# Expert gates built once and parked in DRAM, a longer lead of the u sides, and seven row buffers in a two-block transformer kernel

## The chip, the cores and the metric

One core of a Trainium2 chip runs the whole program in one launch. The metric is device time in microseconds for one execution. The core's engines are TensorE (PE, with its weight loads listed as PEld), VectorE (DVE), ScalarE (ACT), GpSimd (POOL) and SyncE (SP), and 16 DMA engines move data between DRAM and the on-chip memory, SBUF.

## What is computed

Two transformer blocks over 512 tokens of width 1024, in float32. The change lies in the first block's expert layer ("PEER"): 16384 experts, one row of `expert_u` and one of `expert_v` each, of which every token uses 16 for each of 8 heads.

```python
def block(xb):
    q = (xb @ w_query).reshape(PEER_TOKEN_BLOCK, PEER_HEADS, 2, PEER_HALF_DIM)
    s = jnp.einsum('chpd,hpnd->chpn', q, sub_keys).astype(jnp.float32)
    top_s, top_i = lax.top_k(s, PEER_TOPK)
    ...
    best_s, pos = lax.top_k(cand_s, PEER_TOPK)
    idx = jnp.take_along_axis(cand_i, pos, axis=-1)
    g = jax.nn.softmax(best_s, axis=-1)
    u = expert_u[idx]
    act = jax.nn.gelu(jnp.einsum('cd,chkd->chk', xb, u).astype(jnp.float32), approximate=False)
    w = (g * act).astype(xb.dtype)
    return jnp.einsum('chk,chkd->cd', w, expert_v[idx])
```

An expert's number is 128 i + j, with i and j the winners of two lists of 128 keys. Attention, norms and the second block's feed-forward are around it and are not touched, but for the buffers of the second block's attention result.

## The kernel before

Float32 products are made of three matmuls on a high and a low part (`mm3`). The high part `wh` of a weight tile is cut by ACT (L111), the low part `wl` by DVE or POOL (L112). Weights come in 256 KB tiles `wr` on SP's DMA queue (L93), a few tiles ahead.

The first 128 tokens take the **rows path**: for each of the 128 (head, choice) pairs, POOL issues an indirect DMA that fetches 128 rows of `expert_u` (`ur`, 512 KB; L1078), DVE multiplies them with the tokens and sums (L1081), and later the same is done with `expert_v` (`vr`), which DVE adds into `acc` (L1089). That makes 256 units; their buffers are the pool `prow`.

The other 384 tokens take the **dense path** over 128 expert blocks of 128 experts; block b holds the experts with i = b. A *u side* is 24 matmuls of 384 columns into PSUM (`pA`; the first twelve, made earlier, are called `pU`), and ACT's gelu. `weigh` (L1044 on) multiplies the result by the block's gates (`w`, DVE) and splits it (`wwh` on ACT, `wwl` on DVE). A *v side* is 18 matmuls of 512 columns into six PSUM banks `vac`, which hold the sum over all blocks.

The **gates** of a block are a 128 x 384 matrix over (j, token), mostly zeros. They are made for 8 tokens at a time (a *group*, 48 in all): DVE compares the chosen j and i with a row of numbers, which gives one-hot tiles `oj` and `oi` (L1000, float16), `oi` times the gate values gives `og` (L1007), and 16 matmuls per group multiply `oj` and `og` (`pG`, L1019 and L1020). ACT copies the result into a buffer `ring` (L1023) of 60 columns of 128 x 384, which the gelu results of the first blocks share. Since the ring does not hold all, the columns i are built in three chunks of 38, 45 and 45 (`CH`): the first before any v side, with ten u sides between; the second and third during the blocks 23 to 36 and 68 to 81 (`build`). In the first chunk every third group has its `og` made on POOL. The u sides lead the v sides by `AHEAD` = 22 blocks.

The main loop runs b over the blocks: u side of block b + 1 (from 22 on), v side of b, `weigh(b + 1)`, and then some gathers of the rows path, as many as the table `share` gives; each is settled by DVE at once. The program order fixes what each engine does in turn, together with a scheduler that orders instructions by when their inputs come; SP's queue holds loads in the order in which they are asked for.

Of the kernel before, what the change touches and what calls it, by code (L numbers as in the profile page):

```python
# [157 lines left out]
def body(ctx, tc, a):  # L158
# [276 lines left out]

    for b in range(P - KL):
        if b + 1 >= AHEAD:
            add_u(b + 1)
        add_v(b)
    for b in range(P - KL + 1, P):  # L440
        add_u(b)
    for b in range(P - KL, P):
# [548 lines left out]
    acc = pac.tile([P, D], FT, name="acc")
    starts = [sum(CH[:c]) for c in range(3)]

    def gate_hot(c, g):

        n, i0 = CH[c], starts[c]
        tt = slice(g * GS, (g + 1) * GS)

        def hot(out, q, j0, w):
            V.tensor_tensor(out, iT[:, q, tt].rearrange("p (s t) -> p s t", t=4)[:, :, None].to_broadcast([P, GS // 4, w, 4]),  # L1000
                            ioth[:, None, j0:j0 + w].to_broadcast([P, GS // 4, w, 4]), op=OP.is_equal)
        oj = pg.tile([P, GS // 4, P, 4], F16, name=f"oj{c}_{g}", tag="oj", bufs=3)
        hot(oj, 1, 0, P)
        oi = pg.tile([P, GS // 4, CW, 4], F16, name=f"oi{c}_{g}", tag="oi", bufs=2)
        hot(oi[:, :, :n], 0, i0, n)
        og = pg.tile([P, GS, 48], FT, name=f"og{c}_{g}", tag="og", bufs=3)
        (G if c == 0 and g % OGP == 0 else V).tensor_tensor(og[:, :, :n].rearrange("p (s t) i -> p s t i", t=4),  # L1007
                        oi[:, :, :n].rearrange("p s i t -> p s t i"),
                        gp32[:, tt].rearrange("p (s t) -> p s t", t=4)[:, :, :, None].to_broadcast([P, GS // 4, 4, n]),
                        op=OP.mult)  # L1010
        return c, g, oj, og

    def gate_sum(c, g, oj, og):
        n, i0 = CH[c], starts[c]
        tt = slice(g * GS, (g + 1) * GS)
        pt = ps.tile([P, GS, CW], FT, name=f"pG{c}_{g}", tag="pG")
        for t in range(GS):
            o = og[:, t, :n].bitcast(F16).rearrange("p (i w) -> p i w", w=2)
            T.matmul(pt[:, t, :n], oj[:, t // 4, :, t % 4], o[:, :, 1], start=True, stop=False)  # L1019
            last["pe"] = T.matmul(pt[:, t, :n], oj[:, t // 4, :, t % 4], o[:, :, 0], start=False, stop=True).ins  # L1020
        s0 = i0 % RING
        n1 = min(n, RING - s0)
        A.activation(ring[:, s0:s0 + n1, tt].rearrange("p i t -> p t i"), pt[:, :, :n1], AF.Copy)  # L1023
        if n1 < n:
            A.activation(ring[:, 0:n - n1, tt].rearrange("p i t -> p t i"), pt[:, :, n1:n], AF.Copy)

    hot = []
    late["tile"] = lambda n, tag, nm: pg.tile([P, n], FR, name=f"late{nm}", tag=tag, bufs=3)

    def gate_group(c, g, lag=2):  # L1030
        hot.append(gate_hot(c, g))
        if len(hot) > lag:
            gate_sum(*hot.pop(0))

    gact = {b: ring[:, CH[0] + b] for b in range(n_early)}

    def u_side(b):
# [3 lines left out]
        gact[b] = ring[:, CH[0] + b] if b < AHEAD else pg.tile([P, TD], FT, name=f"ga{b}", tag="ga")  # L1041
        last["gelu"] = A.activation(gact[b], pa_, AF.Gelu).ins  # L1042

    def weigh(b):  # L1044
# [1 line left out]
        V.tensor_mul(w, gact.pop(b), ring[:, b % RING])  # L1046
        if b < P - 2:
            wh, wl = (pg.tile([P, TD], FR, name=f"ww{c}{b}", tag=f"ww{c}") for c in "hl")
        elif b == P - 2:
            wh, wl = (late["tile"](TD, "og", f"w{c}") for c in "hl")  # L1050
        else:
            wh, wl = (pk.tile([P, TD], FR, name=f"late{c}", tag=c) for c in ("gp", "iT"))
# [4 lines left out]
    def v_side(*v):  # L1057

        for t in range(3):
            sl = slice(t * P, (t + 1) * P)  # L1060
            for b, wh, wl, vb in v:
                for n in range(2):
                    if hot and 2 * t + n in GAT:
                        with tc.issue_after(last["pe"]):
                            gate_sum(*hot.pop(0))
                    last["pe"] = mm3(vac[2 * t + n], wh[:, sl], wl[:, sl], vb[n][0], vb[n][1], b == 0, b == P - 1)
# [39 lines left out]
    NG = TD // GS  # L1106
    for i in range(NG):
        gate_group(0, i)
        NU = n_early
        if i * (AHEAD - NU) // NG != (i + 1) * (AHEAD - NU) // NG:  # L1110
            u_side(NU + i * (AHEAD - NU) // NG)
    while hot:
        gate_sum(*hot.pop(0))
# [4 lines left out]
    build = {}
    for c, (w0, w1) in ((1, (max(AHEAD, CH[0] + CH[1] - RING), CH[0] - 1)), (2, (P - RING, CH[0] + CH[1] - 1))):
        for i in range(NG):  # L1120
            build.setdefault(w0 + i * (w1 - w0) // NG, []).append((c, i))
    share = [SH_BUILD if b in build else (SH_EARLY if b < AHEAD else (SH_MID if b < 64 else SH_LATE if b < B_END else 0)) for b in range(P)]
    scale = len(units) / sum(share)
    due, done = 0.0, 0
# [460 lines left out]
```

## Time and profile before

| | us |
|---|---|
| median of 3 runs | 2203.68 (2198.78 to 2205.65) |
| the profiled execution | 2202.07 |
| its span | 2200.3 |
| PE busy in the span | 2090.5 |
| DVE busy | 1603.3 |
| ACT busy | 955.0 |
| POOL busy | 622.6 |

The profile is of one execution. The span is the time from the first to the last instruction. A matmul counts as busy from its start to its modelled end, so PE shown busy may still be at half its rate; the granted clock (PEclk, as a share of 2.4 GHz) tells which. The expert layer's stages follow one another: gates of the first chunk with ten u sides, v sides alone, the second chunk among u and v sides, u and v sides, the third chunk, u and v sides again, and a tail.

### The profile page before, as it was taken

To read this page: it belongs to the slowest core of one execution; us is meant where nothing else is said; L and a number is where in the kernel's file an instruction comes from. 1 tells how busy PE (TensorE), PEld (TensorE's weight loads), DVE (VectorE), ACT (ScalarE), POOL (GpSimd) and SP (SyncE) were. 2 spreads that over 40 slices of the span, in tenths; PEclk is the share of its full clock that TensorE was granted. 3 is DMA by queue.
4 is the path that set the end of the run, shared out by engine and by line. 5 is a ranking of instruction groups with operands and counts; after the bars stand their busy time and mean duration, and the time that the engine had idled before them with its cause. 6 is when DMAs were issued, how large, how long until landed. Compare 5 with 4: busy or idle time off the path is not lost.

```text
span 2200.3 us, 34912 instructions
## 1 busy us (share of the span) xinstructions
PE 2090.5 (95%) x12443; PEld 1768.9 (80%) x12443; DVE 1603.3 (73%) x3498; ACT 955.0 (43%) x1892; POOL 622.6 (28%) x537
## 2 busy tenths in 40 slices
PE   8999998978999999999999999999999999999999
PEld 5756787878888888888888878788878678888887
DVE  8789879988878987777899777777777855333322
ACT  4477342355445553333455433333453554333321
POOL 2245236664221123333311233333212420000000
PEclk9999999999999999999999999999999899999999
DMA  8525422331675558888855688888743121233332
GB/s 280 163 59 182 153 73 78 100 101 59 217 227 193 168 191 270 278 275 278 273 180 170 202 269 278 269 275 278 276 147 119 56 63 53 97 96 96 97 119 72
DMA packets 163633, 375.78 MB, mean 171 GB/s; under 512 B 18562, under 2 KB 22530, under 8 KB 163459
## 3 DMA queue, kind: packets, MB, share of 16 engines
q1 hardware_dynamic: 121058, 233.81, 31.9%
q0 software_dynamic: 36864, 134.23, 19.4%
q10 hardware_dynamic: 5536, 5.51, 0.9%
q8 instruction: 98, 1.61, 0.3%
q14 instruction: 77, 0.62, 0.1%
HBM read 366.66 MB, written 4.19 MB: 169 GB/s over the span
## 4 chain that ended last, share of the span: by engine, by line
PE 62%; DVE 14%; DMA 12%; issue 5%; ACT 3%; POOL 3%; SPq 0%; DVEq 0%; ACTq 0%; POOLq 0%
PE vac L200 5%; PE vac L199 5%; PE vac L201 5%; PE pA L199 4%; PE pA L200 4%; PE pA L201 4%; DMA vr<-in_v_dram,idx 4%; DMA ur<-in_u_dram,idx 3%; DMA wr<-in_uT_dram 3%; DMA wr<-in_v_dram 2%; PE pd L201 2%; PE pd L200 2%; PE pd L199 2%; PE upp L201 2%; PE upp L199 2%
## 5 line engine op out<-in xcount | busy, mean ns | idle before, releaser
L111 ACT ACTIVATE wh<-wr 128x512 fp32r<-128x512 f32 x716 | 447.8, 631 | 769.8 <-DMA wr<-in_v_dram 133.7
L112 DVE TENSOR_TENSOR wl<-wr,wh 128x512 fp32r<-128x512 f32 x640 | 429.9, 697 | 280.8 <-ACT wh L111 261.4
L200 PE MATMUL vac<-wl,wwh 128*128 128x512 f32 x756 | 305.2, 404 | 33.9 <-DVE wl L112 33.9
L199 PE MATMUL pA<-hA,wh 128*128 128x384 f32 x928 | 316.9, 342 | 0.0
L201 PE MATMUL pA<-hA,wl 128*128 128x384 f32 x928 | 313.8, 338 | 0.0
L200 PE MATMUL pA<-hA,wh 128*128 128x384 f32 x928 | 312.6, 337 | 0.0
L199 PE MATMUL vac<-wh,wwh 128*128 128x512 f32 x756 | 305.0, 404 | 0.6 <-ACT wwh L1053 0.5
L201 PE MATMUL vac<-wh,wwl 128*128 128x512 f32 x756 | 299.1, 396 | 0.1
L1078 POOL DMA_INDIRECT ur<-in_u_dram,idx x128 | 159.5, 1246 | 378.4 <-DVE acc L1089 304.1
L1078 POOL DMA_INDIRECT vr<-in_v_dram,idx x128 | 157.5, 1230 | 339.2 <-DVE ur L1081 265.3
L200 PEld LDWEIGHTS vac<-wl,wwh 128*128 128x128 f32 x756 | 144.6, 191 | 69.4 <-DVE wl L112 45.6
L1089 DVE SCALAR_TENSOR_TENSOR acc<-vr,act,acc 128x1024 f32<-128x1024 f32 x127 | 162.8, 1282 | 44.1 <-DMA vr<-in_v_dram,idx 42.9
L1081 DVE SCALAR_TENSOR_TENSOR ur<-ur,hn 128x1024 f32<-128x1024 f32 x128 | 156.3, 1221 | 43.5 <-DMA ur<-in_u_dram,idx 43.5
L199 PEld LDWEIGHTS pA<-hA,wh 128*128 128x128 f32 x928 | 176.2, 190 | 3.7 <-ACT ga L1042 0.3
L200 PEld LDWEIGHTS pA<-hA,wh 128*128 128x128 f32 x928 | 176.2, 190 | 3.1
L201 PEld LDWEIGHTS pA<-hA,wl 128*128 128x128 f32 x928 | 175.6, 189 | 0.0
L201 PEld LDWEIGHTS vac<-wh,wwl 128*128 128x128 f32 x756 | 144.3, 191 | 31.1 <-DVE wwl L1054 0.5
L199 PEld LDWEIGHTS vac<-wh,wwh 128*128 128x128 f32 x756 | 144.6, 191 | 28.7 <-ACT wwh L1053 0.6
L112 POOL TENSOR_TENSOR wl<-wr,wh 128x512 fp32r<-128x512 f32 x76 | 102.4, 1359 | 74.4 <-ACT wh L111 71.8
L1053 ACT ACTIVATE wwh<-w 128x384 fp32r<-128x384 f32 x126 | 66.0, 524 | 113.7 <-DVE w L1046 107.2
L1019 PEld LDWEIGHTS <-oj 128*128 128x128 f16 x1152 | 83.2, 117 | 38.3 <-issue 15.9
L1000 DVE TENSOR_TENSOR oj<-iT,ioth 128x1024 f16<-128x1024 f16 x144 | 106.5, 743 | 9.3 <-PE pG L1020 9.3
(697 smaller groups left out, 4294.3 us busy)
## 6 DMA issues: line engine op xcount, KB each, us to landing
wr<-in_uT_dram SPq DMA_DIRECT2D x256, 256.0 KB
wr<-in_v_dram SPq DMA_DIRECT2D x256, 256.0 KB
wa<-in_w_adaT_dram SPq DMA_DIRECT2D x48, 512.0 KB
wr<-in_w_gate_dram SPq DMA_DIRECT2D x44, 256.0 KB
wr<-in_w_up_dram SPq DMA_DIRECT2D x44, 256.0 KB
wr<-in_w_down_dram SPq DMA_DIRECT2D x44, 256.0 KB
wr<-in_w_in_dram SPq DMA_DIRECT2D x36, 256.0 KB
wr<-in_w_out_dram SPq DMA_DIRECT2D x32, 256.0 KB
```

The lines of the kernel that those rows point to most:

```text
L111: self.nc.scalar.activation(hi, raw, AF.Copy)
L112: (lo_eng or self.nc.vector).tensor_tensor(lo, raw, hi.bitcast(FT), op=OP.subtract)
L199: T.matmul(out, lh, rh, start=start, stop=False)
L200: T.matmul(out, lh, rl, start=False, stop=False)
L201: return T.matmul(out, ll, rh, start=False, stop=stop).ins
L1000: V.tensor_tensor(out, iT[:, q, tt].rearrange("p (s t) -> p s t", t=4)[:, :, None].to_broadcast([P, GS // 4, w, 4]), ioth[:, None, j0:j0 + ...
L1019: T.matmul(pt[:, t, :n], oj[:, t // 4, :, t % 4], o[:, :, 1], start=True, stop=False)
L1053: A.activation(wh, w, AF.Copy)
L1078: G.indirect_dma_start(out=r, out_offset=None, in_=a[kind], in_offset=bass.IndirectOffsetOnAxis(ap=idx[:, j:j + 1], axis=0))
L1081: V.scalar_tensor_tensor(r, r, 1.0, hn, op0=OP.mult, op1=OP.mult, accum_out=act[:, j:j + 1])
L1089: V.scalar_tensor_tensor(acc, r, act[:, j:j + 1], acc, op0=OP.mult, op1=OP.add)
```

## The change

All 128 columns of gates are built in one phase, group by group, with 22 u sides between (blocks 12 to 33). `oj`, `oi` and `og` are now 1024 elements wide per partition; `oj` and `og` have two buffers, `oi` one. ACT copies a group's two halves into a stage of 64 tokens (`st`), and after every eight groups SP's queue writes the stage, 4.19 MB, to the DRAM tensor `gates`; there are six such stores. In the main loop `gate_load` reads one block back (`gt`, 128 x 6 x 64, pieces of 64 numbers), three blocks ahead, also on SP's queue, into four buffers. The gelu results live in a buffer of 36 (`acts`), and the u sides lead by 34 blocks; the last 34 blocks have no u side beside them. The low parts of the u weights up to there are cut by POOL. The weighed tiles `wwh`, `wwl` have five buffers each instead of two.

The rows path has seven buffers instead of three, and a unit is settled when five later ones have been issued. The 256 units are spread evenly over the blocks up to 119. The second block's `mix2` is in two parts. The tail has four v sides and no u sides, where it had three u sides too.

```diff
-CH = (38, 45, 45)
-CW = max(CH)
-RING = 60
+AA = 36
+AHEAD = 34
+ST = 64
+ROWS, LAG = 7, 5
+OGB = 2
-    pr = pool(s1, "prow", 3)
+    def gate_hot(g):
...
+        oj = pg.tile([P, GS // 4, P, 4], F16, name=f"oj{g}", tag="oj")
+        hot(oj, 1)
+        oi = pg.tile([P, GS // 4, P, 4], F16, name=f"oi{g}", tag="oi", bufs=1)
+        hot(oi, 0)
+        og = pg.tile([P, GS, P], FT, name=f"og{g}", tag="og")
+        (G if g % OGP == 0 else V).tensor_tensor(og.rearrange("p (s t) i -> p s t i", t=4),
...
+    def gate_sum(g, oj, og):
+        n, t0 = divmod(g * GS, ST)
+        if t0 == 0:
+            stage[n] = pg.tile([P, P, ST], FT, name=f"st{n}", tag="st", bufs=2)
+        for h in range(GS // 4):
+            pt = ps.tile([P, 4, P], FT, name=f"pG{g}_{h}", tag="pG")
+            for t in range(4):
+                o = og[:, 4 * h + t].bitcast(F16).rearrange("p (i w) -> p i w", w=2)
+                T.matmul(pt[:, t], oj[:, h, :, t], o[:, :, 1], start=True, stop=False)
+                T.matmul(pt[:, t], oj[:, h, :, t], o[:, :, 0], start=False, stop=True)
+            A.activation(stage[n][:, :, t0 + 4 * h:t0 + 4 * h + 4].rearrange("p i t -> p t i"), pt, AF.Copy)
+        if t0 + GS == ST:
+            nc.sync.dma_start(gd[n], stage.pop(n))
...
+    for i in range(NG):
+        hot.append(gate_hot(i))
+        if len(hot) > 1:
+            gate_sum(*hot.pop(0))
+        for b in range(n_early + i * (AHEAD - n_early) // NG, n_early + (i + 1) * (AHEAD - n_early) // NG):
+            u_side(b)
...
+    pr = pool(s1, "prow", ROWS)
+    def gate_load(b):
+        gates[b] = pg.tile([P, TD], FT, name=f"gt{b}", tag="gt", bufs=4)
+        nc.sync.dma_start(gates[b].rearrange("p (n t) -> p n t", t=ST), gd[:, :, b].rearrange("n j t -> j n t"))
...
+        V.tensor_mul(w, acts[:, b % AA], gates.pop(b))
+        wh, wl = (pg.tile([P, TD], FR, name=f"ww{c}{b}", tag=f"ww{c}", bufs=KL + 1) for c in "hl")
...
     for b in range(P - KL):
-        nb = [gate_hot(c, i) for n, (c, i) in enumerate(build.get(b, [])[:2])]
-        if b + 1 >= AHEAD:
-            u_side(b + 1)
+        if b + 3 < P:
+            gate_load(b + 3)
+        if b + AHEAD < P:
+            u_side(b + AHEAD)
         v_side((b, *wts, [ws.get(("v", b, n)) for n in range(2)]))
         wts = weigh(b + 1)
+        due = min(len(units), -(-(b + 1) * len(units) // B_END))
+        with tc.issue_after(last["w"]):
+            while done < due:
                 gather(*units[done])
+                done += 1
+                if len(rows) > LAG:
+                    settle(*rows.pop(0))
```

In the gate phase POOL has the low parts of u weights and every third `og` in one list. Before, in the phase of the first chunk (`og_0` is chunk 0; the number after a name is its instance):

```order
L1078 DMA ur_6938<-in_u_dram,idx 128x1024
L112 TENSOR_TENSOR wl_5365<-wr_5183,wh_5364 128x512
L1007 TENSOR_TENSOR og_3_5320<-oi_3_5318,gp 128x8x38
L112 TENSOR_TENSOR wl_5371<-wr_5189,wh_5370 128x512
L112 TENSOR_TENSOR wl_5523<-wr_5221,wh_5522 128x512
L1007 TENSOR_TENSOR og_6_5430<-oi_6_5428,gp 128x8x38
L112 TENSOR_TENSOR wl_5529<-wr_5227,wh_5528 128x512
```

The same place on POOL after:

```order
L1003 TENSOR_TENSOR og_5276<-oi_5274,gp 128x1024
L112 TENSOR_TENSOR wl_5218<-wr_5117,wh_5217 128x512
L112 TENSOR_TENSOR wl_5224<-wr_5123,wh_5223 128x512
L112 TENSOR_TENSOR wl_5332<-wr_5183,wh_5331 128x512
L112 TENSOR_TENSOR wl_5338<-wr_5189,wh_5337 128x512
L1003 TENSOR_TENSOR og_5373<-oi_5371,gp 128x1024
L112 TENSOR_TENSOR wl_5422<-wr_5221,wh_5421 128x512
```

POOL's `og` is over three times as wide and stands between two to four `wl`; the gathers have left the phase.

On SP's queue, where the gate phase ends, weight loads were in one unbroken row before. After, with the last of the six stores:

```order
L93 DMA wr_7404<-in_v_dram 128x512
L93 DMA wr_7410<-in_uT_dram 128x512
L1023 DMA gates<-st_7018 128x8192
L93 DMA wr_7442<-in_uT_dram 128x512
L93 DMA wr_7448<-in_v_dram 128x512
L93 DMA wr_7486<-in_v_dram 128x512
L1048 DMA gt_7386<-gates 128x6x64
L1048 DMA gt_7388<-gates 128x6x64
L1048 DMA gt_7390<-gates 128x6x64
```

The same queue before, in the blocks after the first chunk:

```order
L93 DMA wr_7685<-in_uT_dram 128x512
L93 DMA wr_7691<-in_v_dram 128x512
L93 DMA wr_7724<-in_v_dram 128x512
L93 DMA wr_7730<-in_uT_dram 128x512
L93 DMA wr_7763<-in_uT_dram 128x512
```

The store and the first gate loads stand in SP's list between the weight loads, and each waits there for its own condition.

On DVE in the blocks with u and v sides, a unit of the rows path (`acc`, `ur`) followed its gather at once. Before:

```order
L1054 TENSOR_TENSOR wwl_15420<-w_15417,wwh_15419 128x384
L1089 SCALAR_TENSOR_TENSOR acc<-vr_15423,act,acc 128x1024
L1081 SCALAR_TENSOR_TENSOR ur_15426,act<-ur_15426,hn 128x1024
L1089 SCALAR_TENSOR_TENSOR acc<-vr_15429,act,acc 128x1024
L112 TENSOR_TENSOR wl_15433<-wr_15352,wh_15432 128x512
L112 TENSOR_TENSOR wl_15439<-wr_15358,wh_15438 128x512
L112 TENSOR_TENSOR wl_15472<-wr_15391,wh_15471 128x512
L112 TENSOR_TENSOR wl_15478<-wr_15397,wh_15477 128x512
L1046 TENSOR_TENSOR w_15501<-ga_15469,ring 128x384
```

After, in such a block:

```order
L1091 SCALAR_TENSOR_TENSOR acc<-vr_8382,act,acc 128x1024
L112 TENSOR_TENSOR wl_8344<-wr_8265,wh_8343 128x512
L1083 SCALAR_TENSOR_TENSOR ur_8461,act<-ur_8461,hn 128x1024
L1052 TENSOR_TENSOR w_8701<-acts,gt_8467 128x384
L112 TENSOR_TENSOR wl_8350<-wr_8271,wh_8349 128x512
L112 TENSOR_TENSOR wl_8388<-wr_8309,wh_8387 128x512
L1055 TENSOR_TENSOR wwl_8704<-w_8701,wwh_8703 128x384
L112 TENSOR_TENSOR wl_8394<-wr_8315,wh_8393 128x512
L1091 SCALAR_TENSOR_TENSOR acc<-vr_8464,act,acc 128x1024
```

The row operations stand one by one between the splits, about two to a block, and use rows asked for several units earlier.

## Rows read from the trace of the kernel before

**Rows 1.** Page, part 1: busy us (share of the span) and instructions of each engine.

```profile
PE 2090.5 (95%) x12443; PEld 1768.9 (80%) x12443; DVE 1603.3 (73%) x3498; ACT 955.0 (43%) x1892; POOL 622.6 (28%) x537
```

**Rows 2.** Windows: us, busy of PE, PEld, DVE, ACT, POOL; PEclk; DMA share; GB/s.

```profile
455.00:553.00 98.00, 86.42 (x1069) 80.60 (x1067) 80.67 (x142) 52.15 (x89) 49.66 (x39) 0.92 0.27 84
...
825.00:1085.00 260.00, 244.77 (x1196) 217.46 (x1195) 197.57 (x296) 96.85 (x174) 95.63 (x79) 0.98 0.83 275
1245.00:1580.00 335.00, 316.30 (x1557) 282.36 (x1557) 254.95 (x374) 126.03 (x225) 127.36 (x103) 0.98 0.84 279
1643.00:2200.00 557.00, 540.65 (x2723) 440.01 (x2721) 268.25 (x506) 200.24 (x363) 55.83 (x51) 0.98 0.28 87
```

**Rows 3.** Windows: four blocks without a stall, and v sides alone.

```profile
1544.22:1577.45 33.23, 33.23 (x170) 30.26 (x168) 28.31 (x37) 14.16 (x25) 14.71 (x11) 1.00 0.87 303
560.00:620.00 60.00, 60.00 (x264) 49.23 (x263) 49.60 (x90) 24.00 (x45) 14.47 (x14) 1.00 0.80 251
```

**Rows 4.** Window in a rebuild, tile pG alone: us, PE busy, ACT busy, PEclk, DMA, GB/s.

```profile
700.00:800.00 100.00, 22.66 (x512) 26.52 (x64) 1.00 0.54 169
```

**Rows 5.** Timeline of PE: start, us, instruction; the first and the last vac matmul.

```profile
552.92 0.50 PE L199 MATMUL vac<-wh,wwh 128*128 128x512 f32 x1 [0.47 <-ACT wwh L1053]
...
1644.08 0.40 PE L201 MATMUL vac<-latev,lateiT 128*128 128x512 f32 x1
```

**Rows 6.** Waits in 825:1085: engine, line, releaser; us in total, times, longest.

```profile
POOL ur L1078 <- DVE acc L1089: 92.5, 28, 5.9
...
PEld vac L200 <- DVE wl L112: 20.7, 14, 3.2
DVE acc L1089 <- DMA vr<-in_v_dram,idx: 19.5, 15, 2.2
```

**Rows 7.** Chain in 864:878, one of seven pieces alike after a stop: start, us, what.

```profile
874.10 0.43 PE vac L199
```

**Rows 8.** Groups on DVE in 825:1085: count, busy us, mean ns, idle before.

```profile
L112 DVE TENSOR_TENSOR wl<-wr,wh 128x512 fp32r<-128x512 f32 x116 | 74.0, 691 | 9.5 <-ACT wh L111 5.8 <-DMA wr<-in_v_dram 3.1 <-issue 0.3
L1089 DVE SCALAR_TENSOR_TENSOR acc<-vr,act,acc 128x1024 f32<-128x1024 f32 x40 | 51.3, 1282 | 20.2 <-DMA vr<-in_v_dram,idx 19.5 <-DVE ur L1081 0.7
L1081 DVE SCALAR_TENSOR_TENSOR ur<-ur,hn 128x1024 f32<-128x1024 f32 x40 | 48.9, 1222 | 16.1 <-DMA ur<-in_u_dram,idx 16.1
...
L1046 DVE TENSOR_TENSOR w<-ga,ring 128x384 f32<-128x384 f32 x29 | 16.0, 553 | 0.0
```

**Rows 9.** Groups on DVE and POOL in the gate phase, 455:553.

```profile
L1000 DVE TENSOR_TENSOR oi<-iT,ioth 128x304 f16<-128x304 f16 x48 | 20.6, 443 | 7.6 <-POOL og L1007 7.4
L1007 DVE TENSOR_TENSOR og<-oi,gp 128x304 f32<-128x304 f16 x32 | 20.4, 638 | 0.0
...
L112 POOL TENSOR_TENSOR wl<-wr,wh 128x512 fp32r<-128x512 f32 x20 | 29.3, 1463 | 17.7 <-ACT wh L111 15.2 <-PE pG L1020 2.3
L1007 POOL TENSOR_TENSOR og<-oi,gp 128x304 f32<-128x304 f16 x16 | 17.9, 1116 | 24.1 <-DVE oi L1000 12.8 <-PE pG L1020 11.3
```

**Rows 10.** Timeline of DVE and POOL in 487:492; in brackets idle time and releaser.

```profile
489.79 1.40 DVE L1000 TENSOR_TENSOR oi<-iT,ioth 128x304 f16<-128x304 f16 x1 [1.86 <-POOL og L1007]
...
489.04 0.72 POOL L1007 TENSOR_TENSOR og<-oi,gp 128x304 f32<-128x304 f16 x1
489.71 1.31 POOL L112 TENSOR_TENSOR wl<-wr,wh 128x512 fp32r<-128x512 f32 x1
```

**Rows 11.** Chain in 505:520, undisturbed steps of DVE.

```profile
511.12 0.60 DVE oj L1000
511.72 0.23 DVE oi L1000
...
515.84 0.40 DVE og L1007
```

**Rows 12.** Windows: a 64 KB load alone, and DMA at its fullest.

```profile
286.90:287.70 0.80, 0.80 (x6) 0.80 (x5) 0.80 (x2) 0.00 (x0) 0.00 (x0) 0.50 0.28 82
1550.00:1555.00 5.00, 5.00 (x27) 4.53 (x26) 4.37 (x6) 1.16 (x2) 1.52 (x2) 1.00 1.02 399
```

More of the change, by code (lines that the diff above doesn't have):

```diff
@@ L44 @@
 FNV = (1, 3)
-GAT = (3,)
 GSCALE = 4096.0
@@ L433, in add_v @@
                          (P - 1, 0): lambda: [late["h0"][:, i, 4:8] for i in range(2)],
-                         (P - 1, 1): lambda: [late["tile"](512, "oj", f"v{i}") for i in range(2)]}.get((b, c)))
-    for b in range(P - KL):
-        if b + 1 >= AHEAD:
[L438 to L442, printed above, removed]
+                         (P - 1, 1): lambda: [late["tile"](512, f"v{i}") for i in range(2)]}.get((b, c)))
+    for b in range(P):
+        if b + AHEAD < P:
+            add_u(b + AHEAD)
         add_v(b)
@@ L991, in body @@
[L991 to L1035, printed above, removed]
+    pg = pool(s1, "pgb", OGB)
     def u_side(b):
@@ new lines, in body @@
+    stage = {}
+    def gate_sum(g, oj, og):
[11 more added lines that the diff above has]
+            nc.sync.dma_start(gd[n], stage.pop(n))
@@ new lines, in body @@
+    hot = []
+    NG = TD // GS
+    for i in range(NG):
[4 more added lines that the diff above has]
+            u_side(b)
+    while hot:
+        gate_sum(*hot.pop(0))
+    s1.close()
+    s1 = ExitStack()
+    pg = pool(s1, "pg", 2)
+    pr = pool(s1, "prow", ROWS)
+    pac = pool(s1, "pac")
+    act = pac.tile([P, P], FT, name="act")
@@ L1044, in weigh @@
+    acc = pac.tile([P, D], FT, name="acc")
+    late["tile"] = lambda n, nm: pac.tile([P, n], FR, name=f"late{nm}")
+    gates = {}
+    def gate_load(b):
+        gates[b] = pg.tile([P, TD], FT, name=f"gt{b}", tag="gt", bufs=4)
+        nc.sync.dma_start(gates[b].rearrange("p (n t) -> p n t", t=ST), gd[:, :, b].rearrange("n j t -> j n t"))
     def weigh(b):
         w = pg.tile([P, TD], FT, name=f"w{b}", tag="w", bufs=1)
[L1046 to L1052, printed above, removed]
+        V.tensor_mul(w, acts[:, b % AA], gates.pop(b))
+        wh, wl = (pg.tile([P, TD], FR, name=f"ww{c}{b}", tag=f"ww{c}", bufs=KL + 1) for c in "hl")
@@ L1062, in v_side @@
                 for n in range(2):
[L1063 to L1066, printed above, removed]
+                    mm3(vac[2 * t + n], wh[:, sl], wl[:, sl], vb[n][0], vb[n][1], b == 0, b == P - 1)
     units = []
@@ L1074, in body @@
     units += [("v", j) for j in range(P - GU, P)]
+    rows = []
     def gather(kind, j):
@@ L1079, in gather, with settle @@
                              in_offset=bass.IndirectOffsetOnAxis(ap=idx[:, j:j + 1], axis=0))
+        rows.append((kind, j, r))
+    def settle(kind, j, r):
         if kind == "u":
@@ L1104, in final_norm @@
         return rstd(ss[:, 0:1], 1, 1.0 / D, f"f{b}")
[L1106 to L1113, printed above, removed]
     t = ps.tags
-    ps = ps.then((*t["rest"], *t["pA"][:2], *t["pG"][:2], t["pA"][2], t["pG"][2]),
-                 **{f"vac{i}": 1 for i in range(6)}, pA=1, pG=1)
+    ps = ps.then((*t["rest"], *t["pG"], *t["pA"]), **{f"vac{i}": 1 for i in range(6)}, pG=1, pA=1)
     vac = [ps.tile([P, 512], FT, name=f"vac{i}", tag=f"vac{i}") for i in range(6)]
[L1118 to L1124, printed above, removed]
+    for b in range(3):
+        gate_load(b)
     wts = weigh(0)
+    done = 0
     for b in range(P - KL):
-        nb = [gate_hot(c, i) for n, (c, i) in enumerate(build.get(b, [])[:2])]
-        if b + 1 >= AHEAD:
-            u_side(b + 1)
-        for g in nb:
-            hot.append(g)
-        for n, (c, i) in enumerate(build.get(b, [])[2:]):
-            gate_group(c, i)
+        if b + 3 < P:
+            gate_load(b + 3)
+        if b + AHEAD < P:
+            u_side(b + AHEAD)
         v_side((b, *wts, [ws.get(("v", b, n)) for n in range(2)]))
-        while hot:
-            gate_sum(*hot.pop(0))
         wts = weigh(b + 1)
-        due += share[b] * scale
-        while done < min(len(units), round(due)):
-            with tc.issue_after(last["w"]):
+        due = min(len(units), -(-(b + 1) * len(units) // B_END))
+        with tc.issue_after(last["w"]):
+            while done < due:
                 gather(*units[done])
-            done += 1
+                done += 1
+                if len(rows) > LAG:
+                    settle(*rows.pop(0))
+            while rows and done == len(units):
+                settle(*rows.pop(0))
         if b == B_END:
@@ L1356, in beside @@
             yield
-        for m in W2ORDER[6 + U_PRE:]:
-            pool_tile(m)
-            yield
         while todo:
```

45 lines of the change are left out of this document (25 added, 20 removed).

## The prediction, made before the changed kernel was run

> **What bounds the kernel now.** I read the page's busy line first: TensorE (PE) is busy 95% of the span [rows 1]. The table of windows by stage says where the other 5% and the PE work itself lie [rows 2]: PE is busy 86 of 98 us while the first gates are built, 245 of 260 and 316 of 335 in the two stretches where expert blocks run with u and v sides together ("dense stretches"), and 541 of 557 after the expert stage, which the change hardly touches. The expert stage proper runs from the first vac matmul at 552.92 to the last at 1644.3 [rows 5], 1091.4 us.
>
> What should it take? Four blocks without a stall took 33.23 us, 8.31 us for one u side and one v side. In 560:620 nothing but v sides runs: 264 matmuls in 60 us, 0.227 us each, 18 to a block, 4.10 us per v side [rows 3]. So a u side is 4.21 us. A gate matmul of 45 columns is 22.66 us / 512 = 44 ns [rows 4], and 1536 of them lie in the stage, 68 us. Sum: 106 u × 4.21 + 128 v × 4.10 + 68 = 1039 us. About 53 us are lost, and all of the loss must be stalls and half-speed matmuls. The first dense stretch holds 29 blocks by its w operations [rows 8], 8.97 us each against 8.31. The waits of the same 260 us show the cause [rows 6]: the u gathers on POOL waited 92.5 us for the accumulation on VectorE (DVE) that frees one of three row buffers, DVE waited 19.5 us for v rows, and PE's loads 20.7 us for wl splits that stood behind them on DVE. After such a stop, PE runs vac matmuls at 0.43 us each, the pace of the lower clock of 1.2 GHz against 0.23 [rows 7].
>
> **The change part by part.**
>
> *1. Removed from the expert stage:* both gate rebuilds, 1536 × 44 ns = **−68 us** of PE, plus their one-hot work on DVE (which was beside PE). All of it was on PE's path there, since PE is the engine that is full.
>
> *2. The stage has fewer u sides:* 24.9 u sides past the twelve early ones stand before the first vac matmul on PE's list, against 10 before. About 92 remain: 92 × 4.21 + 128 × 4.10 = **912 us** of PE work.
>
> *3. Gate phase longer.* Before, it ran from 455 to 552.9, 98 us. Its DVE and POOL operations do not overlap: with POOL's wl split running from 489.71 for 1.31 us, a DVE oi that takes 0.23 elsewhere took 1.40 and ended as POOL did [rows 10, 11]. So I add the two engines. Test on before: 48 oj × 0.60 + 48 oi × 0.23 + 32 og × 0.40 on DVE, 16 og × 0.72 + 20 wl × 1.31 on POOL [rows 9 to 11] = 90 us of the 98, a factor of 0.92. After: oi now has the size of oj (0.60), og is 1024 elements instead of 304. On DVE I take 1.2 for it (between 1.0 and 0.40 × 1024/304 = 1.35; twice oj's 0.60 for twice its output bytes), on POOL 0.72 × 3.37 = 2.4. DVE: 96 × 0.60 + 32 × 1.2 = 96. POOL: 16 × 2.4 + 44 wl (22 u sides, all splits on POOL) × 1.31 = 96. Sum 192, by 0.92 = **208 us**, so the phase ends at 663. Bounds: 192 with no gap at all, 226 at a factor of 0.85. PE's own work there, 22 × 4.21 + 768 × 0.058 (44 ns scaled by the extra columns at most to 58) = 137 us, is covered; it would only bind if the two engines overlapped, which rows 10 exclude. It needs a mean clock of two thirds at least.
>
> The single oi buffer adds a wait: after each og on POOL the next oi waits for POOL, and behind it on DVE stand the og and oj of later groups. As the two exclude each other anyway, I cost this at nothing beyond the factor. The cover is gone if POOL's og itself waits behind a wl whose weights are late. That can come from SyncE: each of six 4.19 MB stores waits on its queue for ACT's last evacuation of 64 tokens, with weight loads queued behind. A store is 10.5 us at the 399 GB/s of [rows 12]; two u sides of weights are in hand, and a u side comes every 9.5 us here.
>
> *4. Turn from gates to blocks (new).* The first w cannot start before the last store has landed and a gate block has come back: store 10.5 us, and w with its two splits, three operations near the 0.55 of w [rows 8], 1.7. For two evacuations, the fixed part of two transfers and one load no row of this pairing exists: 2 to 15 us, I take 7. Sum **19 us**, during which PE has 2.9 u sides (12 us, counted in part 2). First vac near 682, against 552.9. A store at half that rate adds 10.
>
> *5. Gate blocks read back.* Per block 768 pieces of 256 B. The nearest row is a load of 64 KB in 128 pieces of 512 B: 0.8 us × 0.28 × 16 engines / 128 = 28 ns each [rows 12]. Half the bytes: 14 to 28 ns, so 0.67 to 1.34 us of every DMA engine per block. Loads, gathers and gates of a u+v block are by their shapes 1.05 + 1.12 + 0.20 = 2.36 MB, 285 GB/s at 8.31 us; four blocks ran at full PE rate under 303 [rows 3]. So it is hidden, up to (8.31 − 2.17/0.399) × 16/768 = 60 ns per piece. The loads sit on SyncE's queue: a gate load waits for its buffer, freed by the w four blocks back, and weight loads queue behind it; they are three blocks, 25 us, ahead. I cost this at nothing.
>
> The Trainium skill (DMA: Bandwidth & Descriptors, Specifications) speaks against this part: it asks for transfers of at least 512 B for line rate, with a read-modify-write below. Its section on latency and other measured facts adds that row pitches at large powers of two halve the rate; the gates tensor has 32 KiB between partitions and 4 MiB between token groups. No row here shows either; if both held, the 28 ns would double at most twice, which is rival B.
>
> *6. Gathers with seven buffers and a lag of five.* Each gather has some 5 units to land instead of being settled next. A block carries 2.13 of them instead of 80/29 = 2.76 [rows 8]. DVE needs 4 × 0.69 + 2 × 0.56 + 2.13 × 1.29 = 6.6 us of 8.31 [rows 8]; a buffer comes round every 7/2.13 × 8.31 = 27 us against 3/2.76 × 8.97 = 9.8. Of the 53 us the dense stalls should go. I leave 0.1 per u+v block, 9 us.
>
> *7. What is late next:* blocks 94 to 119 now have no u side, so PE wants one every 4.10 us, while DVE needs 2 × 0.69 + 1.12 + 2.13 × 1.29 = 5.25 and DMA 1.64 MB / 0.399 = 4.1 plus 0.67 to 1.34. I take 5.4 per block. With weights, rows and gates some four blocks ahead (five ww buffers) it costs 22 × 5.4 − 26 × 4.1 = 12 us; without that lead 34. I take 15, and 5 for the last blocks.
>
> *Sum:* 682 + 912 + 9 + 15 + 5 = 1623 for the end of the vac matmuls, against 1644.3: **−21 us**. The 556 us behind stay. The changed buffers of the second block's mixer move no matmul there; I cost them at 0 to 3. Span 2179 and execution 2181 against 2200.3 and 2202.07; the median of the runs was 1.6 above the profiled one, so the forecast is **2182 us**.
>
> **The rivals.**
>
> *A, slower: the gate phase is a chain.* With two oj/og buffers, one oi and POOL's og behind wl splits, handing over costs more than the factor of before. A triple of groups (two og on DVE, one on POOL) is 13.0 us in my sum; sixteen triples make each extra us cost 16. From 229 us of phase (14.3 per triple) nothing is gained. At 15 the phase takes 240 and the time is 2214. For it: DVE's waits on POOL's og in rows of before, with two oi buffers [rows 10], and PE's lower load, 137 of 208 us, which may bring the lower clock; against: exclusion makes most of such waits cost nothing twice.
>
> *B, slower: gate reads bound the blocks.* At 100 ns a piece (four times the 512 B row less a little) they take 4.8 us: a u+v block becomes 5.4 + 4.8 = 10.2, +1.9 × 92, a late v block 8.9, +3.5 × 22: 2182 + 175 + 77 = 2434. It decides from 60 ns. Only the rule above speaks for it.
>
> *C, no change: the blocks keep their stalls.* If gathers, weight loads and reads at 285 GB/s meet as they did, the loss stays 53 instead of 29: 2206. For it: the dense stretches had DMA at 275 to 279 GB/s [rows 2] and lost 0.66 us per block. Against: a full-rate stretch at 303.
>
> **How the numbers follow.** Forecast 0.58, A 0.15, B 0.10, C 0.17. The forecast's own range: phase at 192 and losses of 15 instead of 29 give 2152, with 3 for the turn 2149; a phase of 218 and a turn 5 longer give 2197. A and C reach to 2240 (C with a phase of 226 and a store at half rate: 2206 + 18 + 10 = 2234). So 2149 to 2240, B outside. A difference of 0.3%, 6.6 us, is what a measurement can tell. Faster: the forecast less 0.03 at its upper end, plus 0.02 of C: 0.57. Same: most of C and that end, 0.17. Slower: A, B and a little of C, 0.26.
>
> **What the trace would show.** Gate phase about 208 us with DVE plus POOL filling it; first vac near 682; u+v blocks at 8.3 to 8.4 us under some 285 GB/s with no 0.43 us vac matmuls; late v blocks between 4.1 and 5.6; POOL no longer waiting on DVE's accumulation. I am wrong if the phase passes 229 us, if gate pieces pass 60 ns, or if DVE still waits for rows.

## The result and the profile after

The changed kernel takes 2165.62 us (median of 4 runs, 2163.34 to 2167.05) against 2201.23 before (4 runs): ratio 0.9837, 95% interval 0.9813 to 0.9860, some 36 us less. The forecast was 2182, the range 2149 to 2240: the side and the range held, and the time came out 16 us below the forecast.

The page's busy line answers to [rows 1]. PE is busy 39 us less than before, POOL 35 us more:

```profile
PE 2051.1 (95%) x10907; PEld 1751.0 (81%) x10907; DVE 1516.6 (70%) x3186; ACT 925.5 (43%) x1748; POOL 657.5 (30%) x561
```

The windows by stage answer to [rows 2] (columns: us; busy of PE, PEld, DVE, ACT, POOL; PEclk; DMA share; GB/s). They are the gate phase, the turn, the first blocks, the u+v blocks, most of the late v blocks, and what follows the expert stage:

```profile
456.00:644.00 188.00, 162.99 (x1354) 156.79 (x1353) 145.85 (x135) 131.41 (x174) 102.98 (x61) 0.93 0.49 184
644.00:662.00 18.00, 12.53 (x61) 11.10 (x60) 4.84 (x8) 4.43 (x8) 4.15 (x5) 0.93 0.97 352
662.00:697.00 35.00, 32.10 (x144) 27.64 (x143) 24.97 (x44) 12.58 (x23) 11.69 (x10) 0.94 0.98 315
697.00:1428.00 731.00, 730.25 (x3693) 664.58 (x3692) 528.63 (x829) 284.23 (x535) 221.61 (x192) 1.00 0.89 290
1433.00:1560.00 127.00, 114.44 (x489) 90.30 (x488) 110.04 (x166) 46.60 (x85) 56.76 (x48) 0.99 1.00 337
...
1605.00:2164.00 559.00, 542.24 (x2719) 441.26 (x2717) 266.96 (x510) 199.61 (x363) 54.41 (x51) 0.98 0.27 87
```

In 697:1428 PE is busy 730 of 731 us at the full clock: the stalls of [rows 2] are gone, at 290 GB/s. In 1433:1560 the DMA share is 1.00 and PE idles 12.6 us. The timeline of PE gives the first and the last vac matmul, as [rows 5]:

```profile
661.56 0.63 PE L199 MATMUL vac<-wh,wwh 128*128 128x512 f32 x1
...
1605.16 0.39 PE L201 MATMUL vac<-latev,wwl 128*128 128x512 f32 x1
```

Term by term, in us:

| term | forecast | measured |
|---|---|---|
| gate phase ends | 663 | 643.8 |
| turn to the first vac matmul | 19 | 17.8 |
| PE's work from there | 912 | 907 |
| loss in u+v blocks | 9 | 7 |
| loss in late v blocks and tail | 20 | 30 |
| last vac matmul ends | 1623 | 1605.4 |
| what follows | 556 | 559 |

The losses are read so: from 661.6 to 1605.4 are 943.8 us. In them start 2187 u matmuls, which are 91.1 u sides of 4.21 us, and 2304 vac matmuls of 0.227 us. That is 907 us of work, so 37 us are lost. The last u side ends at 1432.9, and 629 vac matmuls start after it: 143 of 172.5 us, so 30 of the 37 are lost there. The other 7 fell nearly all into the first ten blocks.

**The gate phase.** Groups on DVE and POOL in 456:644 (count, busy us, mean ns, idle before and its releaser), as [rows 9]:

```profile
L996 DVE TENSOR_TENSOR oi<-iT,ioth 128x1024 f16<-128x1024 f16 x48 | 53.9, 1123 | 30.7 <-POOL og L1003 30.2
L996 DVE TENSOR_TENSOR oj<-iT,ioth 128x1024 f16<-128x1024 f16 x48 | 51.4, 1071 | 5.9 <-PE pG L1020 5.9
L1003 DVE TENSOR_TENSOR og<-oi,gp 128x1024 f32<-128x1024 f16 x32 | 43.2, 1351 | 0.3
...
L112 POOL TENSOR_TENSOR wl<-wr,wh 128x512 fp32r<-128x512 f32 x44 | 68.3, 1561 | 41.0 <-ACT wh L111 40.9
L1003 POOL TENSOR_TENSOR og<-oi,gp 128x1024 f32<-128x1024 f16 x16 | 33.9, 2116 | 34.7 <-DVE oi L996 32.0 <-PE pG L1020 2.7
```

Two stretches of the chain of waits in 520:545 (start, us, what) show the undisturbed times and a step that POOL holds up:

```profile
524.97 0.60 DVE oj L996
525.58 1.14 DVE og L1003
526.71 0.60 DVE oj L996
527.31 0.61 DVE oi L996
...
528.12 1.91 POOL og L1003
...
530.05 1.77 DVE oi L996
531.82 1.71 DVE oj L996
```

An oi or oj takes 0.60 undisturbed and 1.7 when POOL is at work; og is 1.14 on DVE and 1.91 on POOL. With a split (wl) at 0.69 on DVE [rows 8] and 1.30 on POOL (1.31 in [rows 10]), the sum of both engines by these times is 96 × 0.60 + 32 × 1.14 + 5 × 0.69 + 16 × 1.91 + 44 × 1.30 = 185 of the 188 us.

**The turn.** The chain in 636:700: the last store took 12.1 us, and the later gate loads, asked for together with gathers and weights, 13.0:

```profile
643.78 12.08 DMA gates<-st
...
657.52 12.98 DMA gt<-gates
```

**The gate reads.** In 658:659 nearly only gate pieces moved. The DMA view of that microsecond:

```profile
DMA packets 982, 0.27 MB, mean 273 GB/s; under 512 B 966, under 2 KB 966, under 8 KB 982
...
q1 hardware_dynamic: 982, 0.27, 118.4%
```

1.184 us × 16 engines / 982 packets is 19 ns a piece by its records, so about 0.9 us of each engine per block, in the middle of the forecast's 14 to 28 ns. (A share above 100% comes from overlapping records; by the clock, 1 us × 16 / 982, it is 16 ns.)

### The profile page after: what moved, and what is told of

The parts are those of the page before. It is cut to its first block, busy times and chain, and to the rows that moved or that the text cites. A ratio compares the mean times of both kernels' runs of the same rounds, so it can differ in the third digit from the quotient of the medians.

```text
span 2164.4 us, 31580 instructions
## 1 busy us (share of the span) xinstructions
PE 2051.1 (95%) x10907; PEld 1751.0 (81%) x10907; DVE 1516.6 (70%) x3186; ACT 925.5 (43%) x1748; POOL 657.5 (30%) x561
## 4 chain that ended last, share of the span: by engine, by line
PE 67%; DVE 17%; DMA 6%; issue 3%; ACT 3%; POOL 2%; SPq 0%; ACTq 0%; POOLq 0%; DVEq 0%
PE pA L199 6%; PE pA L200 6%; PE pA L201 6%; PE vac L200 6%; PE vac L201 6%; PE vac L199 6%; DMA wr<-in_v_dram 2%; PE pd L201 2%; PE pd L199 2%; PE pd L200 2%; PE upp L199 2%; PE upp L200 2%; PE upp L201 2%; PE gatep L200 2%; PE gatep L199 2%
## 5 line engine op out<-in xcount | busy, mean ns | idle before, releaser
L112 DVE TENSOR_TENSOR wl<-wr,wh 128x512 fp32r<-128x512 f32 x616 | 425.2, 694 | 434.9 <-ACT wh L111 431.6
L199 PE MATMUL vac<-wh,wwh 128*128 128x512 f32 x759 | 299.3, 394 | 15.8 <-ACT wwh L1054 13.8
L200 PE MATMUL vac<-wl,wwh 128*128 128x512 f32 x759 | 299.6, 395 | 1.1 <-DVE wl L112 1.1
L1077 POOL DMA_INDIRECT ur<-in_u_dram,idx x128 | 151.0, 1180 | 335.2 <-DVE acc L1091 275.0
L1077 POOL DMA_INDIRECT vr<-in_v_dram,idx x128 | 147.7, 1154 | 297.9 <-DVE ur L1083 266.5
L112 POOL TENSOR_TENSOR wl<-wr,wh 128x512 fp32r<-128x512 f32 x100 | 141.1, 1424 | 98.2 <-ACT wh L111 97.9
L1021 ACT ACTIVATE st<-pG 128x512 f32<-128x512 f32 x96 | 94.2, 1125 | 13.0 <-PE pG L1020 12.9
L1019 PE MATMUL pG<-og,oj 128*128 128x128 f16 x384 | 53.6, 231 | 25.0 <-DVE og L1003 17.6
```

Source lines behind the costliest of these rows:

```text
L112: (lo_eng or self.nc.vector).tensor_tensor(lo, raw, hi.bitcast(FT), op=OP.subtract)
L199: T.matmul(out, lh, rh, start=start, stop=False)
L200: T.matmul(out, lh, rl, start=False, stop=False)
L1019: T.matmul(pt[:, t], oj[:, h, :, t], o[:, :, 1], start=True, stop=False)
L1021: A.activation(stage[n][:, :, t0 + 4 * h:t0 + 4 * h + 4].rearrange("p i t -> p t i"), pt, AF.Copy)
L1077: G.indirect_dma_start(out=r, out_offset=None, in_=a[kind], in_offset=bass.IndirectOffsetOnAxis(ap=idx[:, j:j + 1], axis=0))
```

## The experiments

The theory as predicted had three parts: the stalls go because of the seven buffers and the lag; DVE and POOL share the gate phase one after the other; gate reads are hidden until the late blocks, which DMA bounds. Each ratio below is to the kernel before, run beside that run; where the intervals of two runs overlap, their difference is not told from noise.

**Row buffers back to three.**

```diff
-ROWS, LAG = 7, 5
+ROWS, LAG = 3, 0
```

> The changed kernel with three row buffers and every unit settled when its gather is issued, as before; all else stays (gates from DRAM, 34 blocks of lead, 2.13 gathers per block). Theory, buffers: with 3 buffers a buffer must come round in 3/2.13 x 8.31 = 11.7 us, and a gather takes up to 9 us plus 1.3 of DVE and 1.2 of issue, so DVE waits for rows again; u+v blocks go from 8.31 to 8.6 to 8.95 us, 92 blocks give 27 to 59 us, time 2193 to 2225. Rival, rate: the stalls of before came from 2.76 gathers per block and from the rebuilds; at 2.13 three buffers are enough: u+v blocks 8.31 to 8.4, time 2165 to 2174.

Measured: 2174.9 (ratio to before 0.9858, 0.9806 to 0.9909), some 9 us over the changed kernel, with overlapping intervals. Its u+v blocks:

```profile
755.00:1427.00 672.00, 672.00 (x3399) 611.88 (x3399) 483.24 (x751) 260.37 (x491) 206.76 (x173) 1.00 0.87 286
```

PE never stops. The rival held: the buffers are not what removed the stalls. They gain nothing in the first blocks either: from the first vac matmul to the end of the last u side both kernels take 771 us. This trace is longer by 6 us in the late v blocks (179 against 173) and by 3 behind the expert stage (562 against 559). That the buffers are the cause of this is not shown.

**Seven buffers without the lag.**

```diff
-ROWS, LAG = 7, 5
+ROWS, LAG = 7, 0
```

> The changed kernel with seven row buffers, but each unit settled where its gather is issued. Theory, buffers alone: POOL's gathers wait only for a free buffer, so POOL runs ahead by itself and the place of the settling in DVE's list matters little: 2163 to 2170, u+v blocks 8.31. Rival, the lag does it: DVE stands at the settling for a gather that was just issued (some 5 to 9 us), with the splits behind it; u+v blocks above 8.6, time above 2190.

Measured: 2160.18 (0.9797, 0.9754 to 0.9840), no slower than with the lag. POOL runs ahead by itself: in 697:1428 its gathers wait for DVE to free a buffer, and DVE waits for no row. At this rate the lag adds nothing; in this trace the late v blocks take 161 us without it, against 173.

**The kernel before, gathers spread evenly.**

```diff
-SH_BUILD, SH_EARLY, SH_MID, SH_LATE = 1.5, 1.0, 3.0, 3.0
+SH_BUILD, SH_EARLY, SH_MID, SH_LATE = 1.0, 1.0, 1.0, 1.0
```

> The kernel before with its gathers spread evenly over the blocks up to 119 (2.13 per block everywhere; the table of shares set to 1), nothing else. The run with three row buffers has shown that the buffers are not what removed the stalls. Theory now, rate: 2.76 gathers per block were what DVE could not hold beside a u and a v side, 2.13 is little enough even with three buffers and two ww buffers: u+v blocks outside the rebuilds fall from 8.97 to 8.35 to 8.5 us; the early v-only blocks pay up to 1.2 us each for twice the gathers; time 2170 to 2195. Rival, lead: what removed them is that w and its splits no longer hang on a u side made in the same block (34 blocks of lead, five ww buffers): u+v blocks stay at 8.8 to 9.1, time 2200 to 2225.

Measured: 2194.22 (0.9956, 0.9933 to 0.9978). The early v blocks and the two dense stretches, to be set beside [rows 2]:

```profile
553.00:664.00 111.00, 90.51 (x360) 68.02 (x361) 91.73 (x153) 31.96 (x59) 46.51 (x40) 0.97 0.80 268
847.00:1096.00 249.00, 249.00 (x1261) 226.85 (x1260) 186.85 (x287) 102.65 (x182) 82.37 (x64) 1.00 0.79 265
1250.00:1566.00 316.00, 316.00 (x1612) 287.79 (x1612) 233.96 (x347) 130.66 (x234) 104.76 (x80) 1.00 0.78 262
```

With one line changed, and three buffers, both dense stretches run without a gap. PE idled 15 of 260 and 19 of 335 us in them before, and ran at half speed after each gap. So in this kernel the stalls came with the rate of 2.76 gathers per block. Only some 10 us are gained in all. The early v blocks now carry over twice the gathers, and PE is idle 20 of 111 us there, where [rows 3] had none in 560:620.

**The high rate, in the changed kernel with three buffers.**

```diff
-ROWS, LAG = 7, 5
+ROWS, LAG = 3, 0
...
-B_END = 120
+B_END = 93
```

> The changed kernel with three row buffers, no lag, and the 256 units spread over the blocks up to 92, 2.75 per block, the rate of the dense stretches before. Theory, rate times buffers: the stalls of before come back, u+v blocks 8.6 to 9.0 us, time 2195 to 2225 less some 20 us since no gathers are left for the last blocks: 2175 to 2205. Rival, lead: with w far ahead of its block the rate does no harm, u+v blocks 8.31 to 8.4, time 2145 to 2165.

Measured: 2170.59 (0.9852, 0.9815 to 0.9890). The first eighteen u+v blocks, and the next forty-six:

```profile
687.00:866.00 179.00, 158.43 (x759) 140.17 (x757) 138.15 (x212) 59.50 (x113) 71.54 (x61) 0.96 0.93 308
867.00:1250.00 383.00, 382.61 (x1932) 347.49 (x1932) 311.47 (x469) 150.52 (x280) 145.94 (x127) 1.00 0.97 323
```

Neither theory holds alone. The stalls are back at first (PE busy 158 of 179), then 2.75 gathers per block with three buffers run at full rate, at 323 GB/s; some 3 us of gaps come back between 1250 and 1465. In the kernel before, the same rate with as many buffers did not run at full rate.

**The same rate with seven buffers and the lag.**

```diff
-B_END = 120
+B_END = 93
```

> The changed kernel with its 256 units spread over the blocks up to 92 (2.75 per block), seven row buffers and the lag of five kept. It stands against the same rate with three buffers (2170.59, stalls in the first 20 u+v blocks and a few later). Theory, buffers pay at this rate: the later stalls vanish, u+v blocks 8.31 after a slow start, the late v blocks run at 4.1 to 4.3: 2138 to 2155. Rival, DMA: with 2.75 gathers a block asks 2.69 MB, 323 GB/s, above the 303 seen at full PE rate; blocks go to 8.5 or more, time 2160 to 2180.

Measured: 2145.83 (0.9742, 0.9712 to 0.9772), 25 us under the run with three. First blocks, the other u+v blocks, late v blocks:

```profile
683.00:794.00 111.00, 103.42 (x506) 91.58 (x505) 95.58 (x151) 41.30 (x77) 52.62 (x43) 0.98 1.02 350
794.00:1434.00 640.00, 640.00 (x3237) 582.98 (x3236) 511.42 (x775) 248.80 (x470) 251.51 (x203) 1.00 0.96 320
1440.00:1560.00 120.00, 120.00 (x537) 99.23 (x537) 68.36 (x129) 50.50 (x99) 0.00 (x0) 1.00 0.61 168
```

Here the seven buffers with the lag pay: from the first vac matmul to the end of the last u side it takes 779 us instead of 804, and the rest is alike. And with no gathers left, the late v blocks have no gap at a DMA share of 0.61: gathers together with loads were too much there, as the forecast put it. Whether DMA or DVE was the bound is not separated, since gathers that are gone relieve both (DVE is busy 68 of 120 us, in the changed kernel 110 of 127); the DMA share of 1.00 there speaks for DMA.

**Two buffers for the weighed tiles** (the last blocks keep three of their own).

```diff
-        wh, wl = (pg.tile([P, TD], FR, name=f"ww{c}{b}", tag=f"ww{c}", bufs=KL + 1) for c in "hl")
+        wh, wl = (pg.tile([P, TD], FR, name=f"ww{c}{b}", tag=f"w{'t' if b > P - KL else 'w'}{c}", bufs=KL - 1 if b > P - KL else 2) for c in "hl")
```

> The changed kernel with two buffers for the weighed tiles in the main loop, as before, instead of five (the tail keeps its own three). Theory, rate: no matter in the u+v blocks, 8.31 to 8.35; the late v blocks lose the lead they had (eight blocks at 4.1 before the DMA bound) at most 10 us: 2164 to 2178. Rival, lead: DVE must split w between two v sides, stalls return, u+v blocks above 8.6, time above 2195.

Measured: 2168.11 (0.9849, 0.9813 to 0.9885), not told apart from the changed kernel. The u+v blocks ran without a gap in its trace; the late v blocks took 180 us instead of 173. If that is the work of the lead that five buffers give, it is worth some 7 us there, where the prediction counted 22 (34 without it, 12 with it).

**POOL's share of og given to DVE, then POOL's wl as well.**

```diff
-        (G if g % OGP == 0 else V).tensor_tensor(og.rearrange("p (s t) i -> p s t i", t=4),
+        V.tensor_tensor(og.rearrange("p (s t) i -> p s t i", t=4),
...
```

> The changed kernel with all 48 og of the gate phase on DVE; POOL keeps the 44 low parts of u weights. Theory, DVE and POOL exclude each other, the phase is their sum: 96 x 0.60 + 48 x 1.14 on DVE and 44 x 1.30 on POOL = 170, against 57.6 + 36.5 + 16 x 1.91 + 57.2 = 182 of the 188 measured: the phase falls to 172 to 178, time 2150 to 2157. Rival, DVE's list is the bound and POOL is beside it: DVE's 32 og become 48, 18 us more: phase 188 to 206, time 2165 to 2184.

Measured: 2143.78 (0.9726, 0.9683 to 0.9770), 22 us under the changed kernel and below the 2150 to 2157 expected. The gate phase:

```profile
456.00:625.00 169.00, 153.94 (x1347) 146.48 (x1346) 160.77 (x149) 130.26 (x170) 80.03 (x44) 0.99 0.54 204
```

DVE gets 18 us more to do and the phase becomes shorter, which side by side it could not. But its last gate matmul ends at 622.9 instead of 641.9, 19 us earlier, and the sum of both engines falls by 12 only, 16 × (1.91 − 1.14). The waits between POOL's og and DVE's oi are gone too, and PE's clock in the phase is 0.99 instead of 0.93; which of these made the other 7 us stays open.

Then the low parts (wl) of the phase as well:

```diff
     for b in range(len(u_at), AHEAD):
-        add_u(b, lo=G)
+        add_u(b, **({"lo": G} if b < n_early else {}))
```

> The changed kernel with all og and all low parts of the u weights of the gate phase on DVE; POOL does nothing there. Theory, DVE and POOL exclude each other and the phase is their sum: 96 x 0.60 + 48 x 1.14 + 48 x 0.69 = 145 us, which meets ACT's 96 x 1.13 + 48 x 0.64 + 22 x 0.47 = 149 and PE's 137: phase 150 to 160 against 188, time 2128 to 2142. Rival, the phase is held by hand-overs and not by the sum (one oi buffer, two oj and og): 165 to 180, time 2143 to 2160. Rival, side by side: the time is that of the run with og alone on DVE or above, 2144 or more.

Measured, with both edits: 2131.41 (0.9675, 0.9646 to 0.9705). The gate phase, with POOL idle:

```profile
456.00:611.00 155.00, 153.05 (x1357) 147.59 (x1356) 146.27 (x195) 130.58 (x175) 1.16 (x1) 0.99 0.62 223
```

155 us instead of 188. PE is busy 153 of them at a clock of 0.99: it is the bound now, with DVE close behind at 146.

**Gate reads, twice.**

```diff
+        nc.sync.dma_start(gates[b].rearrange("p (n t) -> p n t", t=ST), gd[:, :, b].rearrange("n j t -> j n t"))
```

> The changed kernel with every gate block read twice into the same tile, 768 more pieces of 256 B per block. Theory, reads are hidden while u and v sides run (18 ns a piece, 0.86 us of each DMA engine per block; DMA share there 0.89, would be 0.99) and cost only where DMA is the bound, the v blocks 14 to 30 past the last u side: u+v blocks 8.31 to 8.5, about 20 late blocks +0.86: +17 to +35, time 2182 to 2200. Rival, small pieces are near their limit already: u+v blocks 9 or more, time above 2230. Rival, DVE bounds the late blocks: +0 to +5.

Measured: 2356.33 (1.0680, 1.0632 to 1.0727), far outside the theory and where the rival had it, above 2230. But DMA was less busy, not more (0.81 against 0.89), as the window over its u+v blocks says:

```profile
747.00:1580.00 833.00, 732.86 (x3507) 642.29 (x3507) 501.05 (x770) 270.95 (x504) 195.40 (x178) 0.97 0.81 258
```

SyncE's queue shows why (waits in 900:1100: us in total, times, longest):

```profile
SPq L1049 <- DMA gt<-gates: 114.4, 18, 7.9
```

The second load (L1049) into the same tile waited in the queue until the first had landed, 6.4 us each, and the weight loads queued behind. The run prices that wait, not the reads.

**Gate reads of twice the bytes in as many pieces** (the five row buffers make the room):

```diff
-ROWS, LAG = 7, 5
+ROWS, LAG = 5, 3
...
-        gates[b] = pg.tile([P, TD], FT, name=f"gt{b}", tag="gt", bufs=4)
-        nc.sync.dma_start(gates[b].rearrange("p (n t) -> p n t", t=ST), gd[:, :, b].rearrange("n j t -> j n t"))
+        gt = pg.tile([P, TD // ST, 2, ST], FT, name=f"gt{b}", tag="gt", bufs=4)
+        c = min(b, P - 2)
+        gates[b] = gt[:, :, b - c]
+        nc.sync.dma_start(gt, gd[:, :, c:c + 2].rearrange("n j i t -> j n i t"))
...
```

> The changed kernel with gate reads of twice the bytes in as many pieces (a block's 64 numbers and its neighbour's, 512 B), one DMA each as now; five row buffers and a lag of three make the room. The run with two reads per block made SP wait for the first to land before the second, with weight loads behind, so it priced a queue and not the bytes. Theory: a piece goes from 18 to 27 ns, 0.43 us more of each DMA engine per block; u+v blocks stay at 8.31 to 8.4 (DMA share 0.89 to 0.94), some 20 late blocks pay 0.43: +3 to +15 us, 2168 to 2181. Rival, the DMA engines are at their limit in u+v blocks already: these go above 8.6, time above 2195.

Measured: 2175.49 (0.9885, 0.9845 to 0.9925), 10 us over the changed kernel, with intervals that just overlap. That is the size expected, but not the place: in the traces 8 of the 10 us lie before the end of the last u side, in the first blocks, and 2 in the late ones (the two buffers fewer may have a part in it). First blocks and the other u+v blocks, where PE has no gap at a DMA share of 0.93, and then the same first blocks of the changed kernel:

```profile
677.00:755.00 78.00, 68.97 (x338) 59.64 (x336) 59.53 (x102) 27.68 (x53) 29.03 (x25) 1.00 0.99 338
755.00:1428.00 673.00, 672.93 (x3402) 612.89 (x3403) 484.75 (x751) 261.80 (x493) 197.35 (x173) 1.00 0.93 310
...
677.00:755.00 78.00, 74.92 (x370) 67.62 (x369) 63.28 (x107) 30.01 (x57) 30.83 (x26) 0.98 0.97 328
```

**A version from the findings.** POOL idle in the gate phase as above, no lag, and

```diff
-B_END = 120
+B_START, B_END = 6, 104
...
-        due = min(len(units), -(-(b + 1) * len(units) // B_END))
+        due = min(len(units), max(0, -(-(b + 1 - B_START) * len(units) // (B_END - B_START))))
```

> A version put together from the runs: gate phase with POOL idle (og and low parts on DVE), no lag, and the units spread over the blocks 6 to 103 (2.61 per block), so that the first blocks after the gates find the DMA engines free and the late v blocks have no gathers. Theory: 30 to 36 us from the gate phase, 5 to 10 from the first u+v blocks, 10 to 20 from the late ones, with u+v blocks at 8.31 to 8.4: 2105 to 2125. Rival, DMA: 2.61 gathers ask 314 GB/s, blocks go to 8.6 and eat the rest: 2130 to 2145.

Measured: 2104.63 us (0.9563, 0.9536 to 0.9590), 61 us under the changed kernel. In the traces 30 of them lie before the first vac matmul, 3 from there to the end of the last u side, 24 in the late v blocks and 4 behind the expert stage. Gate phase, u+v blocks, late v blocks:

```profile
456.00:613.00 157.00, 152.58 (x1351) 147.11 (x1352) 148.55 (x199) 129.54 (x175) 2.67 (x3) 0.98 0.61 223
672.00:1395.00 723.00, 723.00 (x3658) 658.58 (x3657) 567.92 (x876) 281.34 (x531) 277.18 (x229) 1.00 0.95 317
1400.00:1530.00 130.00, 128.01 (x573) 105.73 (x572) 94.78 (x156) 57.48 (x108) 15.61 (x13) 1.00 0.76 234
```

## Why the prediction was right, and where it was not

1. **Gate matmuls out of the expert stage (step 1) and the PE sum (step 2): right.** From the first vac matmul on, work and losses make up the measured 943.8 us. The work is 907 us and not 912, mostly because the prediction's own count, 128 − 12 − 24.9 = 91.1 u sides, had been rounded to 92.
2. **Gate phase (step 3): mechanism right, size off by 19 us, more than the whole error of the forecast.** Adding DVE and POOL was borne out by giving POOL's work to DVE: the sum fell, and the phase with it, from 188 to 169 and 155, though the first step was 7 us more than the sum gives. Two terms were too large: og on POOL took 1.91, not 2.4 (scaled from 304 elements as if there were no fixed part; 8 us), and the factor of 0.92, taken over from the phase before, was 0.99 here (some 13 us). The bound of 192 "with no gap at all" was thereby passed. The remark that PE would bind if the two engines did not stand in each other's way came true when POOL was emptied; PE was then busy 153 us, not 137.
3. **Turn (step 4): right,** 17.8 against 19. The store took 12.1, not 10.5, and all the rest 5.7, not 8.7.
4. **Reads (step 5): right within its bounds.** 19 ns a piece, hidden beside u and v sides once the first blocks are past; rival B, at 100 ns, fell with it. The Trainium skill's rule of at least 512 B for line rate (DMA: Bandwidth & Descriptors, Specifications) shows here as 273 GB/s for 256 B pieces against 399 in [rows 12], about a third less. The halving that the same page gives for row pitches at large powers of two (Latency and other measured facts) does not show in these 273 GB/s, with 32 KiB between partitions. The 60 ns point was not tested.
5. **Gathers (step 6): the size was right, 7 us of loss left against 9, and the reason given was wrong.** That the size came out was luck as far as the buffers go: the change lowered the rate along with adding them. At 2.13 gathers per block three buffers do as well in u+v blocks, and the kernel before loses its dense stalls by the even rate alone. The step took the waits of POOL on DVE [rows 6] for the cause; but such waits are still there without a stall, in a queue that runs ahead (waits of the changed kernel in 697:1428):

```profile
POOL ur L1077 <- DVE acc L1091: 257.3, 84, 5.8
POOL vr L1077 <- DVE ur L1083: 230.7, 82, 5.5
```

   So the sign named ahead of the run, "POOL no longer waiting on DVE's accumulation", was a bad one. The stalls before needed the high rate; at that rate the changed kernel without its extra buffers stalls mostly in the first eighteen blocks. Whether the longer lead of w or something else carries it later was not separated: two weighed tiles in place of five made no difference in the u+v blocks at 2.13, and were not tried at 2.75.
6. **Late v blocks (step 7): 10 us short.** 30 us are lost, not 20. In kind it fits, with a DMA share of 1.00 and no gap once the gathers end earlier, but DMA and DVE as bounds were not separated.
7. **What follows (0 to 3): 3.** The experiments' traces show 555 to 563 us there, so 3 are within their spread.

So the forecast was close also because terms that were too large (19, 5, 2 and 1 us) and too small (10 and 3) partly cancelled. Of the rivals, A fell with a phase of 188 us, where it needed more than 229. Its hand-overs were not tested by themselves: the runs that give og to DVE take them away together with POOL's work, and the 7 us left open above may be theirs. C fell with the 8.31 us blocks.

## What to carry to other kernels

Read a stall by what is late when it starts, and test the rate before the depth: one line that spread the gathers evenly took the stalls away for which four more buffers were given the credit, and buffers paid only where the rate was high. Two engines that lengthen each other's steps should be added, and then the work goes to the one that does it faster, even if that one has the longer list. In this program a second transfer into a tile waited in the queue for the first, and the loads behind it waited too: price a read by a run in which it has its own place.

## What the runs showed of the hardware

DVE comparisons with two inputs took 0.60 us with POOL idle and 1.7 beside a POOL operation with two inputs, and a split moved from POOL to DVE cost 0.69 instead of 1.30; leaving POOL idle made the phase 33 us shorter. PE ran at its full rate under 323 GB/s (DMA share 0.97), more than the 303 of [rows 3]. DRAM reads in pieces of 256 B took 19 ns each by their records, 273 GB/s over 16 engines, and a store of 4.19 MB 12.1 us, 347 GB/s.
